# Other seeds for the plan that gives the large buffers of a two-layer generator block their SBUF addresses

## The chip, the cores and the metric

The kernel is one program on one core of one Trainium2 chip. The metric is the device time of one execution in microseconds (us); lower is better.

## The reference

Two layers run over 512 latent tokens and 256 context tokens of width 1024, all in 32-bit floats. A layer has two halves:

```
h = modulate(rmsnorm(x)); p = h @ w_in            # q, k, v, pooling and Fourier inputs, four gates
y = neighbourhood attention, differential attention, pooling mixer, Fourier mixer
x = x + gt1 * (sum_i sigmoid(gate_i) * (y_i @ w_br[i])) @ w_o
h2 = modulate(rmsnorm(x)); aff = softmax(h2 @ w_router)
each of 16 experts takes its top 64 latent (32 context) tokens:
x = x + gt2 * scatter_add(g * (silu(xe @ w_gate) * (xe @ w_up)) @ w_down)
```

The last layer drops the context's own mixers and experts. An expert's weights are 3 x 1024 x 1408 floats, 17.3 MB, and are read once per layer.

## The kernel before, in words

Work is traced once without addresses to find out in which order instructions read and write each large buffer. The program is then traced a second time with an address for every large buffer ("Q" tile: weights, raw loads, attention heads, residuals, accumulators). All of them live in one arena of 183296 bytes per partition (L56). Between the two traces a planner (`place`, `place_part`, `fit`, L60 to L125) chooses the addresses. Small tiles come from ordinary pools and are not part of the plan.

The planner knows of each buffer its first and last instruction and its size. `fit` gives a buffer the place whose latest former user ended earliest in the list of instructions, among the places that are free over its whole life; expert weights (22528 bytes, or halves of 11264) go to multiples of their size. `place_part` takes the buffers of one stretch in an order: first those that live for 2000 instructions or more, then by first use. A buffer that finds no place is moved forward at a position that a random generator with the given seed draws, up to 400 times. `place` does this for four stretches in turn, divided by the marks that the program sets: layer 0 up to its second expert's loads; the experts of layer 0 and the start of layer 1; layer 1 from the end of its first projection to its second expert's loads; the experts of layer 1. Each has its seed in `SEEDS` (L57); where that seed finds no placement, seeds 0 to 39 are tried.

An address works on the time through waits alone: the first write into a place waits for the last user of what lay there. For a load that wait is taken by the queue that issues it, and everything behind it on that queue waits too. SP issues most loads, in program order: raw gate weights `craw` (L598), raw output weights `wo_raws` (L402), attention heads (L769 and L770, with POOL; L887 and L888, with ACT), residuals `x_res` (L1408), and expert weights `w_ex` (L1440 for the first ones, the head; L1445 for the rest).

The head is the first expert's gate and up weights in eight quarter loads (A, A, A, A, B, B, B, B), two blocks of the second expert's (1A) and two of the first expert's down weights (0D). They lie end to end over 180224 of the arena's 183296 bytes, and each takes the place of something that the output projection still uses. In layer 1 four of them are issued before the output projection's first pass (L1204), among the loads of `x_res` and `wo_raws`; one more at the start of its second pass (L1380), the others behind it. `queued` (L1429) lets no more than two expert loads be in flight. After the second pass come top-k on VectorE, a gather of token rows by POOL (L1485), the experts' gate and up products (`gu`, L1512, inputs c = 0 to 7, A holds 0 to 3, B 4 to 7) and down products (L1545). The next expert's block takes a place as soon as the two input slices that lay there have been used.

Of the kernel before, what the change touches and what calls it, by code (L numbers as in the profile page):

```python
# [53 lines left out]


ARENA = 183296  # L56
SEEDS = 48, 0, 1, 0  # L57


def lifetimes(instructions, asked):  # L60
# [10 lines left out]
def fit(lives, room, offs, n):  # L71

    a, z, size = lives[n]
    near = [(offs[m], offs[m] + lives[m][2], *lives[m][:2]) for m in offs]
    busy = [(p, e) for p, e, f, t in near if f <= z and t >= a]
    some = {0, room - size} | {e for _, e, _, _ in near} | {p - size for p, _, _, _ in near}
    best = None
    for o in range(0, room - size + 1, size) if size in (4 * WB, 2 * WB) else sorted(some):
        if o < 0 or o + size > room or any(o < e and p < o + size for p, e in busy):
            continue  # L80
        key = max((t for p, e, f, t in near if t < a and p < o + size and o < e), default=-1), o
        if best is None or key < best:
            best = key
    return best and best[1]


def place_part(lives, room, part, seed, done, tries=400):

    rnd = random.Random(seed)
    order = sorted(part, key=lambda n: (lives[n][1] - lives[n][0] < 2000, lives[n][0]))  # L90
    for _ in range(tries):
        offs = dict(done)
        for n in order:
            o = fit(lives, room, offs, n)
            if o is None:
                break
            offs[n] = o
        else:
            return offs
        order.remove(n)  # L100
        with_n = [i for i, m in enumerate(order) if m in offs and lives[m][0] <= lives[n][1] and lives[m][1] >= lives[n][0]]
        order.insert(rnd.choice(with_n) if seed and with_n else 0, n)


def place(lives, room, marks):


    done = {}
    for z, (a, b) in enumerate(zip([0] + marks, marks + [len(lives)])):
        for seed in (SEEDS[z], *range(40)):  # L110
            offs = place_part(lives, room, range(a, b), seed, done)
            if offs is not None:
                break
        else:
            raise ValueError("no room")
        done = offs
    return [done[n] for n in range(len(lives))]
# [1700 lines left out]
```

## Time and profile before

| | |
|---|---|
| median of 3 runs | 2738.1 us (2737.04 to 2740.97) |
| the profiled execution | 2742.23 us, span 2740.4 us |
| TensorE (PE) busy | 2429.4 us, 89% of the span |
| VectorE, ScalarE, GpSimd busy | 983.3, 577.4, 474.3 us |
| HBM read and written | 734.01 and 39.58 MB |

A row of the profile gives an engine, a line of the kernel, the tiles written and read, a count and times in us. "PE x <- DMA y" in a list of waits says that PE stood idle before x until the transfer y had landed. SPq, ACTq and POOLq are the queues' own instructions.

### The profile page before, as it was taken

How to read it: one execution, taken by the hardware profiler on the slowest of the kernel's cores; microseconds unless marked ns; L12 is line 12 of the kernel's file. 1: busy time of each engine (PE TensorE's matmuls, PEld its weight loads, DVE VectorE, ACT ScalarE, POOL GpSimd, SP SyncE). 2: the span in 40 equal slices, each digit the busy share in tenths (PEclk: the TensorE clock that was granted, in tenths of full speed). 3: DMA queues.
4: the chain of work that ended last, by engine and by line, in shares of the span. 5: the costliest groups of instructions: out<-in, count | busy, mean ns of one | idle time of the engine just before them, and what ended most of it. 6: DMA issues, size and time to landing. Idle time of an engine off the chain costs nothing. (4 is left out here: it accounts for less than half of the span.)

```text
span 2740.4 us, 48684 instructions
## 1 busy us (share of the span) xinstructions
PE 2429.4 (89%) x21446; PEld 1679.8 (61%) x21446; DVE 983.3 (36%) x1986; ACT 577.4 (21%) x1094; POOL 474.3 (17%) x347
## 2 busy tenths in 40 slices
PE   7989889999969999999997799999974977777776
PEld 5778889999845555677774677877862422222222
DVE  5666547643251111111112765477432110110101
ACT  4324445433310000000001424344320000000000
POOL 1352332211240111111001211011121111010100
PEclk9999999999989999999998899999996999999999
DMA  7673552323379999999997575544369999999997
GB/s 291 194 246 121 174 167 63 104 82 102 118 301 421 414 415 411 412 414 409 414 413 285 171 233 162 170 127 129 119 208 370 420 419 422 417 419 420 419 418 324
DMA packets 131154, 776.74 MB, mean 283 GB/s; under 512 B 13312, under 2 KB 51072, under 8 KB 107136
## 3 DMA queue, kind: packets, MB, share of 16 engines
q1 hardware_dynamic: 113296, 730.38, 68.5%
q0 software_dynamic: 11776, 25.44, 3.9%
q10 hardware_dynamic: 5872, 17.83, 2.1%
q8 instruction: 168, 2.75, 0.4%
q14 instruction: 42, 0.34, 0.0%
HBM read 734.01 MB, written 39.58 MB: 282 GB/s over the span
## 5 line engine op out<-in xcount | busy, mean ns | idle before, releaser
L1512 PE MATMUL gu_ps<-w_ex,xT 128*32 128x352 f32 x10240 | 815.8, 472 | 131.1 <-DMA w_ex<-in_w_ex 93.7
L1512 PEld LDWEIGHTS gu_ps<-w_ex,xT 128*32 128x32 f32 x10240 | 469.9, 112 | 471.2 <-issue 227.0
L616 PE MATMUL gate_ps<-hh,cw 128*128 128x384 f32 (+1 forms) x1536 | 456.2, 364 | 8.7 <-ACT sg L1010 4.6
L1545 PE MATMUL dn_ps<-w_ex,hidT 128*32 128x512 f32 x2816 | 343.7, 596 | 36.9 <-DMA w_ex<-in_w_ex 34.7
L616 PEld LDWEIGHTS gate_ps<-hh,cw 128*128 128x128 f32 x1536 | 287.5, 192 | 34.3 <-issue 5.4
L1521 ACT ACTIVATE hid<-gu_ps 128x352 f32<-128x352 f32 x80 | 37.1, 464 | 1282.4 <-PE gu_ps L1512 1282.4
L616 PE MATMUL gate_ps<-hl,cw 128*128 128x384 f32 (+1 forms) x768 | 277.8, 362 | 0.0
L1545 PEld LDWEIGHTS dn_ps<-w_ex,hidT 128*32 128x32 f32 x2816 | 115.7, 110 | 232.3 <-issue 192.5
L1547 DVE SCALAR_TENSOR_TENSOR y_e<-dn_ps,gval,gt 128x512 f32<-128x512 f32 x32 | 24.0, 751 | 471.2 <-PE dn_ps L1545 471.2
L1522 DVE TENSOR_TENSOR hid<-hid,gu_ps 128x352 f32<-128x352 f32 x80 | 41.7, 521 | 355.8 <-ACT hid L1521 246.6
L616 PEld LDWEIGHTS gate_ps<-hl,cw 128*128 128x128 f32 x768 | 147.6, 192 | 10.6 <-issue 1.5
L173 DVE TENSOR_TENSOR cw<-craw,cw 128x1280 fp32r<-128x1280 f32 (+1 forms) x72 | 116.8, 1626 | 31.2 <-ACT cw L172 30.8
L1526 POOL DMA_INDIRECT out<-y_e,idx x16 | 25.8, 1609 | 586.4 <-DVE y_e L1547 586.4
L1539 DVE SCALAR_TENSOR_TENSOR y_e<-dn_ps,gval,gt 128x256 f32<-128x256 f32 x16 | 7.7, 484 | 308.9 <-PE dn_ps L1537 308.9
L1030 POOL TENSOR_TENSOR acc<-acc,sg 128x384 f32<-128x384 f32 (+1 forms) x48 | 62.5, 1302 | 321.9 <-DVE sg L1020 223.0
L1526 POOL DMA_INDIRECT cs<-y_e,idx x16 | 27.1, 1691 | 494.0 <-DVE y_e L1539 494.0
L1537 PE MATMUL dn_ps<-w_ex,hidT 128*32 128x256 f32 x1408 | 99.5, 379 | 0.0
L172 ACT CAST cw<-craw 128x1280 fp32r<-128x1280 f32 (+1 forms) x72 | 88.9, 1240 | 38.2 <-PE branch_ps L1014 11.0
L282 POOL TENSOR_TENSOR ada_acc<-ada_acc,w_ada_k 128x1024 f32<-128x1024 f32 x28 | 71.5, 2554 | 130.0 <-ACT w_ada_k L281 129.9
L284 DVE SCALAR_TENSOR_TENSOR ada_acc<-w_ada_k,scT,ada_acc 128x1024 f32<-128x1024 f32 x56 | 81.0, 1446 | 33.0 <-DMA w_ada_k<-in_w_ada 31.2
L1010 ACT ACTIVATE sg<-gate_ps 128x384 f32<-128x384 f32 (+1 forms) x96 | 50.5, 526 | 177.6 <-PE gate_ps L616 148.8
L909 DVE TENSOR_REDUCE df_m<-df_s 128x1 f32<-128x768 f32 (+1 forms) x80 | 66.9, 845 | 34.4 <-PE df_s L908 34.3
(347 smaller groups left out, 3198.2 us busy)
## 6 DMA issues: line engine op xcount, KB each, us to landing
w_ex<-in_w_ex SPq DMA_DIRECT2D x176, 2816.0 KB
w_ada_k<-in_w_ada SPq DMA_DIRECT2D x80, 512.0 KB
craw<-in_w_gb SPq DMA_DIRECT2D x64, 640.0 KB
w_ex<-in_w_head SPq DMA_DIRECT2D x16, 1408.0 KB
w_ex<-in_w_head SPq DMA_DIRECT2D x8, 2816.0 KB
qkv_raws<-in_w_qkv SPq DMA_DIRECT2D x12, 768.0 KB
w_ada<-in_w_ada SPq DMA_DIRECT2D x4, 2048.0 KB
wo_raws<-in_w_out SPq DMA_DIRECT2D x8, 768.0 KB
```

The costliest lines, as they stand in the source:

```text
L172: self.nc.scalar.copy(hi, src)
L173: self.nc.vector.tensor_sub(lo, src, hi.bitcast(F32))
L282: nc.gpsimd.tensor_add(a, a, t)
L284: nc.vector.scalar_tensor_tensor(a, t, sc, a, op0=OP.mult, op1=OP.add)
L616: nc.tensor.matmul(ps, w[:, lw, k], self.hT(lh, k, t0, t1), start=(k == 0 and s == 0), stop=(k == 7 and s == 2))
L909: nc.vector.tensor_reduce(st[:, m:m + 1], sp[:, 0:n], axis=AX.X, op=OP.max)
L1010: nc.scalar.activation(sg, pg, AF.Tanh, scale=0.5)
L1030: nc.gpsimd.tensor_add(ac, ac, sg)
L1512: nc.tensor.matmul(PG[e, g][s][32 * j:32 * j + 32], XT[e][:, g, c], self.w_gu(e, c, s, j), start=(c == 0), stop=(c == 7))
L1526: nc.gpsimd.indirect_dma_start(out=x, out_offset=bass.IndirectOffsetOnAxis(ap=idx, axis=0), in_=y, in_offset=None, compute_op=OP.add)
L1537: nc.tensor.matmul(ps[32 * j:32 * j + 32], HT[e][:, 2, k], self.w_dn(e, k, 256 * j, 256 * j + 256), start=(k == 0), stop=(k == 10))
L1545: nc.tensor.matmul(ps[32 * q:32 * q + 32], HT[e][:, g, k], self.w_dn(e, k, 512 * h, 512 * h + 512), start=(k == 0), stop=(k == 10))
```

## The change

Two constants and one sort key. The first and the third of the four seeds change; the second and the fourth stay. With an even seed the order in which buffers are placed starts as before (long-lived first), with an odd seed it starts by first use alone. No instruction of the program is added, removed or moved by the text of the change.

```
 ARENA = 183296
-SEEDS = 48, 0, 1, 0
+SEEDS = 150, 0, 27, 0
...
     rnd = random.Random(seed)
-    order = sorted(part, key=lambda n: (lives[n][1] - lives[n][0] < 2000, lives[n][0]))
+    order = sorted(part, key=lambda n: (seed % 2 == 0 and lives[n][1] - lives[n][0] < 2000, lives[n][0]))
     for _ in range(tries):
```

## Rows read from the trace of the kernel before

**Rows 1.** The page, part 1: busy us and share of the span.
```profile
span 2740.4 us, 48684 instructions
PE 2429.4 (89%) x21446; PEld 1679.8 (61%) x21446; DVE 983.3 (36%) x1986; ACT 577.4 (21%) x1094; POOL 474.3 (17%) x347
```

**Rows 2.** Windows: length, engines' busy us, then clock, DMA share, GB/s.
```profile
823.30:1450.00 626.70, 625.73 (x8229) 407.35 (x8225) 100.86 (x161) 20.42 (x44) 80.10 (x64) 1.00 1.01 414
2101.50:2713.60 612.10, 482.96 (x5267) 183.72 (x5259) 67.36 (x105) 13.90 (x30) 47.47 (x39) 0.96 1.01 420
...
763.00:811.00 48.00, 25.93 (x231) 15.67 (x229) 29.98 (x89) 6.66 (x14) 17.08 (x14) 0.79 0.83 321
2041.50:2101.50 60.00, 23.01 (x180) 15.74 (x183) 21.60 (x72) 5.68 (x13) 20.07 (x14) 0.63 0.88 340
```

**Rows 3.** PE's waits, whole span: us in total, times, longest.
```profile
PE na_s L796 <- DMA na_head<-na_st: 7.3, 3, 3.7
PE df_s L907 <- DMA df_head<-df_st: 4.1, 1, 4.1
PE wo_ps L1380 <- ACT wo_w L172: 9.1, 1, 9.1
PE wo_ps L1380 <- DVE wo_w L173: 0.9, 1, 0.9
```

**Rows 4.** SP's waits, 1640 to 1722 and 1760 to 1786 us.
```profile
SPq L769 <- PE poolw_ps L687: 5.8, 1, 5.8
...
SPq L769 <- PE fnet_wps L739: 4.6, 1, 4.6
...
SPq L887 <- PE branch_ps L1014: 4.8, 1, 4.8
```

**Rows 5.** Timeline of SP, 1900 to 2140 us: start, us, issue.
```profile
1959.33 0.38 SPq L402 DMA_DIRECT2D wo_raws<-in_w_out  x1
1971.65 0.38 SPq L1440 DMA_DIRECT2D w_ex<-in_w_head  x1
1975.99 5.02 SPq L1408 DMA_DIRECT2D x_res<-xs  x8
1981.06 21.68 SPq L1440 DMA_DIRECT2D w_ex<-in_w_head  x3
2002.84 0.94 SPq L402 DMA_DIRECT2D wo_raws<-in_w_out  x2
...
2020.86 63.80 SPq L1440 DMA_DIRECT2D w_ex<-in_w_head  x8
```

**Rows 6.** SP's waits, 1959 to 2013 us.
```profile
SPq L1440 <- DMA w_ex<-in_w_head: 17.6, 1, 17.6
...
SPq L1440 <- PE gate_ps L616: 11.9, 1, 11.9
...
SPq L1408 <- PE branch_ps L1014: 3.9, 1, 3.9
```

**Rows 7.** SP's waits, 2013 to 2102 us.
```profile
SPq L1440 <- PE wo_ps L1380: 24.8, 2, 20.2
```

**Rows 8.** Windows of 5 us, columns as in rows 2.
```profile
1965.00:1970.00 5.00, 5.00 (x24) 4.14 (x23) 1.38 (x2) 0.75 (x2) 0.00 (x1) 1.00 0.00 0
...
2030.00:2035.00 5.00, 5.00 (x27) 3.91 (x27) 3.18 (x5) 1.31 (x4) 1.51 (x2) 1.00 0.03 13
```

**Rows 9.** The page, part 6: size of one quarter load of the head.
```profile
w_ex<-in_w_head SPq DMA_DIRECT2D x16, 1408.0 KB
```

**Rows 10.** POOL's waits, 1980 to 2130 us.
```profile
POOL xg L1485 <- DMA h2s<-h: 24.1, 1, 24.1
```

**Rows 11.** SP's waits, 630 to 830 us.
```profile
SPq L1440 <- PE wo_ps L1380: 32.3, 1, 32.3
```

**Rows 12.** Timelines of SP (2060 to 2105 us) and of PE (2085 to 2130 us).
```profile
2099.72 5.07 SPq L1445 DMA_DIRECT2D w_ex<-in_w_ex  x2
...
2091.80 22.07 PE L1512 MATMUL gu_ps<-w_ex,xT 128*32 128x352 f32 x256 [20.89 <-issue]
```

## The prediction

> **What bounds the kernel now.** I first read the page's first part [rows 1]: TensorE is busy for 89% of the span, but that is a mean over stages with different limits, so I cut the span into windows. In both expert stages (the first two windows of [rows 2]) the 16 DMA engines are busy all the time (share 1.01, at 414 and 420 GB/s) over 627 and 612 us. What follows the moment at which such a stream runs full has a fixed length: those bytes at that rate. In between, TensorE is the busy engine, and a layer's way to its stream is TensorE's work plus its gaps. So a gain must come from one of two things: less idle time of TensorE ahead of a stream, or less idle time of the DMA engines in the run-up to it (the last two windows of [rows 2]): 0.17 of 48 us is 8.2 us in layer 0, 0.12 of 60 us is 7.2 us in layer 1.
>
> The list of TensorE's waits says which gaps an address can have caused. An address acts only through a load that waits for its place. Of the causes in that list, four can be of this kind [rows 3]: attention heads of the neighbourhood branch landing late (7.3 us in three waits), differential heads (4.1 us), and output weights that came late to be split (9.1 and 0.9 us). Together 21.4 us. The other waits are for results of VectorE, ScalarE or POOL, or lie inside the full streams, and no address removes them.
>
> **The change, part by part.** The text adds and removes no instruction. It moves buffers, and each moved load counts by what it waits for, on the queue that it holds up.
>
> *Attention heads.* In layer 1 the first head loads stood in SP's queue until TensorE had finished with the buffers that lay there: 5.8 us for the pooling product, 4.6 us for the Fourier product, 4.8 us for a branch product [rows 4]. These users end just before the heads are needed, so a place that came free longer ago would let the load go that much earlier. Bounds: nothing, if the new places end as late, and 7.3 + 4.1 = 11.4 us [rows 3], if all four gaps close. No row says how many close; I take the middle, **5.7 us**.
>
> *Output weights of layer 1.* SP issues a `wo_raws` load at 1959.3, then stands until 1971.65 with the first quarter of the head (11.9 us, for a gate product), then until 1975.99 with `x_res` (3.9 us, for the last branch product), then puts out three more quarters; the last of these waits 17.6 us for an earlier quarter to land, since only two may be in flight [rows 5, 6]. Only then, at 2002.84, come the next two `wo_raws` loads, and TensorE stands still for 10.0 us in front of the second pass [rows 3]. If the new plan frees `x_res` alone, everything behind it moves up by 3.9 us. If it also frees the first quarter, the DMA engines, which do nothing at 1965 to 1970 [rows 8], take it then, and the whole stall can go. If it frees only the quarter, nothing moves, as `x_res` still holds the queue. Bounds 0 and 10.0; I take the smaller of the two gains, **3.9 us**.
>
> *Head loads behind the output projection, layer 1.* At 2020.86 the fifth quarter goes out and the sixth then waits 20.2 us for a product of the second pass [rows 5, 7], while the DMA engines are nearly idle (0.03 at 2030 to 2035) [rows 8]. Counting sizes in the code, the second pass keeps three `acc_r`, three `wo_w`, two `x_res` and one `rows` of 12288 bytes, 110592 in all; six quarters of 11264 fit beside them, so the sixth need not wait. Its 1408 KB [rows 9] are 1.44 MB, and at 420 GB/s [rows 2] they take 3.4 us out of the busy run-up. POOL's gather waits 24.1 us for a store of token rows to land [rows 10], which looks like more to win; but an earlier gather only brings forward loads that find the DMA engines busy, so the bound is their idle time, 7.2 us. Bounds 0 and 7.2; I take **3.4 us**. [...]
>
> *Layer 0.* There the second pass keeps four `acc_r`, three `wo_w`, two `x_res` and two `rows`: 135168 bytes. Beside them exactly four quarters fit, and the fifth must wait for the pass to end: its 32.3 us wait for a product of that pass [rows 11] stays under any plan. Bounds 0 and the 8.2 us of idle DMA time; I take **0**.
>
> *New waits.* The buffers that make room must lie elsewhere, and the arena is nearly full. A new wait can cost nothing, where another engine's work covers it, up to the price of the slower rival below (7.3 us). The nearest row is the mean head wait, 7.3 / 3 = 2.4 us [rows 3]; I take one such, **2.4 us lost**.
>
> Sum: 5.7 + 3.9 + 3.4 - 2.4 = 10.6 us gained. Against the profiled execution, 2742.2, that makes 2731.6; that execution lies 4.1 us above the median of the runs shown, so against 2738.1 the forecast is 2727.5 us.
>
> **The rivals.**
>
> *All of it goes.* 21.4 us of gaps and 7.2 us of idle DMA time close: 28.6 us, giving 2709.5. For it: every one of these waits names a buffer's late user. Against it: the planner counts instructions and not microseconds, and the arena is full at the end of each output projection, whatever the order.
>
> *The waits change their tile.* Each place that is free early for one load is taken from another, and the total stays: 2738.1. This is also what comes out if the change doesn't do what it says: if seed 150 or 27 finds no placement in 400 tries, the seeds 0 to 39 are tried and an arbitrary plan results; and the planner's order of instructions need not be that in which the queues reach them.
>
> *Slower: halves that do not pair.* The streams' first full blocks need two neighbouring quarters of the head. Now the first block of layer 1 goes out at 2099.72 and both are out by 2104.79, 5.07 us later [rows 12], as soon as the gate and up products have used inputs 0, 1 and then 2, 3. If the new plan sets an A quarter beside a B quarter, the first block waits for input 4. TensorE ends the eight inputs at 2091.80 + 22.07 = 2113.87 [rows 12]; the last four take (2113.87 - 2104.79) / 4 = 2.27 us each, so input 4 is done at 2107.1, 7.3 us after 2099.7, and the whole stream moves back: 2745.4 if nothing else changes. It decides as soon as the second quarter's neighbour is one of B. For it: quarters go to any multiple of 11264 bytes, and nothing in the planner asks for pairs. Against it: quarters that come free together tend to be neighbours.
>
> **How the numbers follow.** A part of the waits goes, as summed: 0.42. All of it: 0.10. No net change: 0.25. Slower, by pairs that fail or by a wait of that size: 0.23. The forecast is the likeliest case, 2727.5; its own range runs from 2716.7 (all 21.4 us of TensorE's gaps) to 2732.6 (5.5 us). The range for all, 2711 to 2748, reaches to just short of the case in which all goes, and takes in the slower case with one new head wait on top (2745.4 + 2.4). About 0.2% (5.5 us) is what a measurement of this kernel can tell from no change. Faster by more than that: the first two cases, 0.52. Within it: 0.25. Slower: 0.23.
>
> **What would show it.** Right: in the list of TensorE's waits the rows for `na_head` and `df_head` shrink to about half, the wait for `wo_w` to about 6 us; SP issues `x_res` of layer 1 without a wait for a branch product; the sixth quarter goes out near 2021 less the shift; both expert streams keep share 1.01 and their lengths. Wrong: a new wait of TensorE for a load that now has none; SP held before a `craw` or `wo_raws` load by a late user; the first full block of a stream waiting for a gate product later in the order; or an order of instructions on PE, DVE or ACT other than before, since then the gaps would be new ones and the sum would be about another program.

## The result and the profile after

The changed kernel took 2726.5 us (median of five runs, 2720.9 to 2729.5) beside 2741.0 for the kernel before (median of five): ratio 0.9949, 95% interval [0.9931, 0.9966], 14.5 us faster. The forecast was 2727.5, a gain of 10.6 us. The profiled execution, 2720.94 us, is the fastest of the five.

First the page of the changed kernel, part 1, then all waits of TensorE, over the whole span, that the forecast had counted.

```profile
span 2719.1 us, 48675 instructions
PE 2412.0 (89%) x21446; PEld 1666.4 (61%) x21446; DVE 979.0 (36%) x1986; ACT 577.8 (21%) x1094; POOL 469.0 (17%) x347
```

```profile
PE wo_ps L1380 <- ACT wo_w L172: 6.9, 1, 6.9
PE na_s L796 <- DMA na_head<-na_st: 4.9, 1, 4.9
...
PE wo_ps L1380 <- DVE wo_w L173: 2.0, 2, 1.1
```

The work is the same (21446 products), but TensorE is busy for 17.4 us less than in [rows 1]. Of the 21.4 us of waits in [rows 3], 13.8 are left: the row for differential heads is gone, the neighbourhood heads wait once (in layer 0) instead of three times, the output weights still cost 6.9 us in one piece. So 7.6 us of waits went, and the two profiled spans differ by 21.3. To find the rest, the span is cut at events that all kernels have (the start of what is called first and the end of what is called last, in the trace; us):

| stretch | before | before, mirrored | changed | changed, mirrored |
|---|---|---|---|---|
| start to layer 0's first full block (L1445) | 823.4 | 820.1 | 818.2 | 819.7 |
| to layer 0's last gate and up product | 650.0 | 651.9 | 652.1 | 651.6 |
| to layer 1's first pooling product | 158.0 | 159.3 | 155.7 | 162.0 |
| **mixers**: to layer 1's last gate product | 343.2 | 342.8 | 327.4 | 325.9 |
| **output and run-up**: to layer 1's first full block | 125.2 | 122.5 | 125.1 | 127.3 |
| to the end | 640.7 | 641.9 | 640.6 | 640.8 |

(The mirrored kernels are the first experiment: the same programs once more.) By the means of the two executions each, the mixers of layer 1 gain 16.4 us, layer 0's way to its stream 2.8, the output stage of layer 1 loses 2.3, and the rest stays within 1 us. The windows of the mixers, first of the kernel before, then of the changed one (length, then busy us of PE, PEld, DVE, ACT, POOL, then clock, DMA share, GB/s):

```profile
1631.34:1974.56 343.22, 328.72 (x1660) 260.31 (x1659) 208.29 (x426) 143.92 (x270) 51.54 (x42) 0.98 0.47 144
```

```profile
1625.98:1953.39 327.41, 322.03 (x1660) 255.09 (x1659) 208.25 (x426) 143.65 (x269) 49.96 (x42) 1.00 0.49 149
```

The same 1660 products: idle time falls from 14.5 to 5.4 us, and the products themselves take 6.7 us less, at a granted clock of 1.00 instead of 0.98. Three stretches at half clock account for nearly all of that: in the kernel before, TensorE's granted clock stood at 0.50 for 3.4 us from 1678, 10.2 us from 1784 and 3.4 us from 1876 us, and it was busy for 13.8 us of them. Products of 128x512 started every 0.43 us there (1791 to 1793 us) and every 0.23 us at a clock of 1.00 (1794 to 1797 us), so that 13.8 x (1 - 0.23/0.43) = 6.4 us are lost to the lower clock, an estimate from these rows; the changed kernel's mixers have no such stretch. The forecast had priced idle time alone.

In the output stage SP's timeline of the changed kernel, and two of its waits from 1917 to 2085 us, answer to [rows 5 to 7]:

```profile
1953.19 5.42 SPq L1408 DMA_DIRECT2D x_res<-xs  x8
1958.72 21.10 SPq L1440 DMA_DIRECT2D w_ex<-in_w_head  x4
1979.91 0.95 SPq L402 DMA_DIRECT2D wo_raws<-in_w_out  x2
...
1997.78 62.86 SPq L1440 DMA_DIRECT2D w_ex<-in_w_head  x8
2078.51 60.27 SPq L1445 DMA_DIRECT2D w_ex<-in_w_ex  x10
```

```profile
SPq L1408 <- PE gate_ps L616: 28.4, 1, 28.4
SPq L1440 <- PE wo_ps L1380: 20.8, 1, 20.8
```

SP now stands 28.4 us at the residual rows until the last gate product, while the DMA engines are nearly idle (share 0.07 from 1925 to 1953 us); everything else is issued behind them, and the sixth quarter waits 20.8 us for a product of the second pass, where it waited 20.2. POOL's wait for the stored token rows, of [rows 10], got longer:

```profile
POOL xg L1485 <- DMA h2s<-h: 27.0, 1, 27.0
```

So most of the time comes from one place, the attention heads of layer 1, and from more than their waits.

### The profile page after: what moved, and what is told of

Its sections match the earlier page's. It is cut to its first block, busy times and chain, and to the rows that moved or that the text cites. A ratio compares the mean times of both kernels' runs of the same rounds, so it can differ in the third digit from the quotient of the medians.

```text
span 2719.1 us, 48675 instructions
## 1 busy us (share of the span) xinstructions
PE 2412.0 (89%) x21446; PEld 1666.4 (61%) x21446; DVE 979.0 (36%) x1986; ACT 577.8 (21%) x1094; POOL 469.0 (17%) x347
## 5 line engine op out<-in xcount | busy, mean ns | idle before, releaser
L1545 PEld LDWEIGHTS dn_ps<-w_ex,hidT 128*32 128x32 f32 x2816 | 114.6, 110 | 238.7 <-issue 200.4
L284 DVE SCALAR_TENSOR_TENSOR ada_acc<-w_ada_k,scT,ada_acc 128x1024 f32<-128x1024 f32 x56 | 73.7, 1316 | 38.3 <-DMA w_ada_k<-in_w_ada 38.1
L1537 PEld LDWEIGHTS dn_ps<-w_ex,hidT 128*32 128x32 f32 x1408 | 62.8, 109 | 24.0 <-issue 2.2
```

Of the source, the lines that this page charges most:

```text
L284: nc.vector.scalar_tensor_tensor(a, t, sc, a, op0=OP.mult, op1=OP.add)
L1537: nc.tensor.matmul(ps[32 * j:32 * j + 32], HT[e][:, 2, k], self.w_dn(e, k, 256 * j, 256 * j + 256), start=(k == 0), stop=(k == 10))
L1545: nc.tensor.matmul(ps[32 * q:32 * q + 32], HT[e][:, g, k], self.w_dn(e, k, 512 * h, 512 * h + 512), start=(k == 0), stop=(k == 10))
```

## The experiments

All plans below are lists of offsets, written into the kernel in place of the planner's answer:

```
-    nc, arrays = build(io_arrays, place(lives, ARENA, marks))
+    nc, arrays = build(io_arrays, PLAN)
```

### Do the bytes themselves matter, and how far does an execution scatter?

```
PLAN[n] = ARENA - plan_before[n] - lives[n][2]
```

> The kernel before with every large buffer moved from offset o to the end of the arena minus o minus its size. Every pair of buffers that shared bytes still does, and the order of the instructions is the same on all five engines. Theory (an address acts only through the wait of a load for its place): 2738 us within 4, ratio to before 0.998 to 1.002, and the same rows in the waits of TensorE, each within 1 us. Rival (the bytes themselves matter, by a bank or a port): off by more than 0.2%, with unequal durations of equal instructions. Beside that, the half-clock stretches of TensorE between 1640 and 1980 us are looked at: if they stand elsewhere than in the trace of before, with the same program, part of the 21.3 us between the two profiled executions is the draw of the execution, and not the change.

Measured: 2738.8 us, ratio 0.9995 [0.9983, 1.0006]. The same overlaps at other bytes take the same time. The stretches are those of the table above; none moves by more than 3.2 us. TensorE's clock between 1640 and 1980 us falls at the same three places as before (0.50 from 1785.0 to 1793.3 us; 0.97 over the mixers, beside 0.98). One expectation missed: the waits did not keep to 1 us. TensorE's waits for `na_head` sum to 3.4 us instead of 7.3, since the longest, 3.7 us, is 1.9 us here and put down to ScalarE; the mixers took as long (342.8 us).

> The changed kernel mirrored in the same way: the same overlaps, the same order of instructions on every engine. Theory: 2726 us within 4, ratio to before 0.993 to 0.997. It is a second look at the changed program: if its profiled execution again shows granted clock 1.00 from the first head product of layer 1 to the last gate product, the full clock there belongs to the change; if stretches at half clock turn up, it was luck.

Measured: 2728.8 us, ratio 0.9972 [0.9960, 0.9984], a smaller gain (10.0 us) than the changed kernel's own 0.9949 (14.5 us), with intervals that just meet, and a hair outside the 0.993 to 0.997 that was expected. By the table the 8.0 us between the two profiled executions lie mostly in layer 1's projections (6.3 us), and order and overlaps are equal there, so 6 us, and not 3.2, is the scatter by which any one stretch must be read. The mixers are as short as in the changed kernel (325.9 us, clock 1.00), so that gain and its full clock belong to the change and not to chance.

### Each seed alone

```
PLAN[n] = plan_after[n] if n < 221 else plan_before[n]
```

> Addresses of the changed kernel for the buffers asked for up to layer 0's gathers (seed 150), those of before from layer 1 on (seed 1, long-lived first). Theory (each seed acts on its own layer): layer 0's first full block goes out near 818.2 us instead of 823.4, layer 1's way from its last expert product of layer 0 to its own first full block stays at 626 us, 2733 to 2736 us in all. Rival (the order of instructions, which is worked out anew, carries the gain over into the other layer): layer 1's way shortens by more than 5 us as well.

(Buffers 0 to 220 are layer 0's, its expert stream with them. In the other half before and after change places.) Measured: 2735.6 us, ratio 0.9988 [0.9977, 1.0000]. Layer 0's first full block goes out at 822.8 us, not near 818.2 as expected, and layer 1's mixers take 340.3 us, as before within the scatter. Layer 1's way is 620.2 us, beside 626.4 in the trace of before and 624.6 in the mirrored one: 4 to 6 us shorter, no more than the scatter, so that the rival isn't excluded.

> The other half: addresses of before for layer 0 (seed 48), those of the changed kernel from layer 1 on (seed 27). Theory: layer 0's first full block near 823.4 us as before, layer 1's way 608 to 612 us instead of 626, 2724 to 2729 us in all; with the other half the two gains add up to the change's. Rival (the gain is one of both together, or sits in layer 0): under 5 us of gain here.

Measured: 2734.8 us, ratio 0.9990 [0.9979, 1.0001]: a miss, since 2724 to 2729 was expected. The mixers did come down, to 326.5 us, but the way to the first pooling product grew to 166.5 us. This pairing of halves has a wait of its own. SP's timeline before, and in this kernel:

```profile
1459.52 0.90 SPq L402 DMA_DIRECT2D qkv_raws<-in_w_qkv  x2
...
1489.67 0.33 SPq L1410 DMA_DIRECT2D xq<-cs  x1
```

```profile
1487.93 0.33 SPq L1410 DMA_DIRECT2D xq<-cs  x1
1488.35 0.86 SPq L402 DMA_DIRECT2D qkv_raws<-in_w_qkv  x2
```

The first two projection weights go out behind the token rows, at which SP stands for 27.2 us, and no longer ahead of them. ScalarE starts to split those weights at 1498.8 us instead of 1476.3. So the shorter mixers are layer 1's seed alone. That this load, with its late turn in the queue, costs all of the 8 us is not shown: the same stretch scattered by 6.3 us at equal order. On this chip the halves gain 3.2 and 4.0 us, and both together, mirrored, 10.0; within the intervals they add up.

### The places or the order of the instructions?

The scheduler that orders the engines' instructions knows the places, so a new plan also gives a new order, and the traces of before and changed do differ in it on all five engines. Two kernels cross them: TensorE and POOL are chained, without any wait for an end, to the order of the other kernel.

```
+    for e, name in order:
+        if e in (mybir.EngineType.PE, mybir.EngineType.Pool,) and name in here:
+            if e in last and (name not in region or region.get(last[e]) != region[name]):
+                tc.add_manual_dep(here[name], last[e], mybir.DependencyInfo(
+                    mybir.DependencyClass.NoSync, mybir.DependencyReason.DATA), reason="order")
+            last[e] = name
```

> Addresses of before; TensorE's and POOL's instructions are held to the order that they have in the changed kernel, the other engines' are worked out anew. Theory (the places themselves bring the gain): the head loads still wait, the stretch of layer 1 from the first pooling product to the last gate product stays near 343 us (343.2 before, 327.4 after), 2736 to 2742 us in all, ratio 0.999 to 1.002. Rival (the other order of TensorE's instructions, which came with the new plan, brings it): that stretch under 333 us, 2724 to 2731 us in all.

> The other way round: addresses of the changed kernel, TensorE and POOL held to the order that they have before. Theory (places): that stretch of layer 1 326 to 330 us, 2724 to 2732 us in all. Rival (order): near 343 us, 2736 to 2742 us in all.

Measured: 2771.0 us, ratio 1.0119 [1.0099, 1.0138], with the old places, and 2754.8 us, 1.0064 [1.0047, 1.0081], with the new ones: both slower than either kernel, and neither theory as it stood. TensorE's waits in the mixers of layer 1 say why; first old places under the new order, then new places under the old order (of the second list the three longest rows):

```profile
PE na_s L796 <- DMA na_head<-na_st: 12.1, 2, 6.1
PE df_s L907 <- DMA df_head<-df_st: 11.1, 2, 6.9
```

```profile
PE df_s L907 <- ACT df_p L912: 9.4, 6, 3.0
PE df_rt L971 <- DVE df_m L910: 1.7, 1, 1.7
PE df_tp L933 <- ACT df_at L935: 1.6, 2, 1.4
```

The new order asks for the heads earlier; over the old places they are then 23.2 us late in all, where the kernel before lost 8.6, and the mixers take 363.7 us. Under the old order the new places do remove every wait for a head there, but TensorE stands idle for 16.5 us, nearly all of it for the softmax on ScalarE and VectorE, and the mixers take 343.9 us, with nothing gained. Five kernels with these places and the order that the scheduler makes for them take 325.9 to 327.9 us. A likely reason, not shown, is that heads that are there early let the scheduler start them early (the first differential product stands 135.1 us behind the first pooling product instead of 149.4), and more gate products are then left to put between the softmax steps.

One limit is large: the other engines' order was worked out anew in these two kernels. In the second one's mixers only 315 of VectorE's 426 instructions stand in the sequence of the kernel before, fewer than the changed kernel's 347, and the 16.5 us are waits for just these engines. In layer 0 both kernels are late too (first full block at 831.2 and 830.8 us, beside 823.4 and 818.2), the second with a wait of 10.9 us for a differential head. So the head waits are the places' doing, but whether TensorE's new order is needed for the gain stays open.

### What does a wait cost beyond its own length?

In the two long waits for heads of the kernel before, products that nobody reads keep TensorE busy; the order of all engines is held.

```
-                H = heads[h2]
+                H = self.busy(heads, h2, (l, pair, u) == (1, 0, units[1]), 1, 15)
...
-                H = heads[h2]
+                H = self.busy(heads, h2, (l, pair, u) == (1, 0, units[1]), 2, 17)
...
+    a, b = heads[0][:, 0, 0:128], heads[0][:, z, 0:T]
+    ps = self.TP("busy_ps")
...
+    for _ in range(n):
+        self.nc.tensor.matmul(ps, a, b, start=True, stop=True)
```

Windows of the kernel before behind those two waits, and of this kernel behind the products that fill them:

```profile
1678.52:1683.00 4.48, 4.48 (x16) 3.80 (x17) 2.41 (x10) 2.13 (x5) 0.00 (x0) 0.69 0.68 266
...
1785.69:1794.00 8.31, 7.63 (x22) 5.71 (x23) 6.87 (x12) 5.63 (x9) 1.29 (x1) 0.50 0.26 93
```

```profile
1680.67:1685.15 4.48, 4.48 (x25) 3.85 (x24) 3.00 (x14) 2.21 (x5) 0.00 (x0) 1.00 0.70 256
...
1786.40:1794.70 8.30, 6.30 (x29) 4.55 (x30) 8.22 (x17) 5.66 (x9) 1.29 (x1) 1.00 0.29 93
```

> The kernel before, all engines held to its order, with products that nobody reads in TensorE's two longest waits for a head load in layer 1: 15 in the 3.67 us ahead of 1678.5, 17 in the 4.11 us ahead of 1785.7, each 0.23 us at full clock, so that they end before the load lands. The waits themselves stay. Theory (a wait costs its idle time and after it a stretch at half clock: 0.69 granted in the 4.5 us behind the first, 0.50 in the 8.3 us behind the second): the clock stays at 1.00 behind both, the stretch from the first pooling product to the last gate product shortens by 4 to 7 us from 343, the whole by as much. Rival (the price of a wait is its idle time alone): no change, that stretch 342 to 344 us; or the products delay the heads' own and it gets longer by up to 3 us.

Measured: 2739.2 us, ratio 0.9996 [0.9985, 1.0007]; mixers 340.6 us. The clock did what was expected, 0.69 and 0.50 became 1.00, so the fall does follow from TensorE standing still ahead of it. The size was a miss: the mixers gained 2.5 us, not 4 to 7, no more than one stretch scatters, and the whole nothing that can be measured. The order is the kernel before's, so its products can be compared one by one, counted from the first pooling product. They run 1.5 us earlier behind the first wait and 3.1 behind the second; 0.4 is lost again at the third fall of the clock, near 1875 us, behind a wait for the softmax that this kernel does not fill (6.8 us at half clock instead of 3.4). The second window shows why it gave back so little: 29 products instead of 22, but VectorE is busy for 8.22 of the 8.30 us, and TensorE, at full clock, stands idle for 2.0 us, most of it for the softmax. An estimate from the kernel before's trace: TensorE was busy at 0.50 for 2.8 us behind the first wait and for 7.6 us behind the second, and by the 0.43 and 0.23 us from one product's start to the next's that is 1.3 and 3.5 us lost to the lower clock. The comparison agrees with it behind the first wait (1.5) and not behind the second (1.6), where the softmax was the next bound.

### The forecast's two other terms, each tried by itself

**Output weights.** In the changed kernel they stand in SP's queue behind four quarters.

```
+        if self.wname == "wo_w" and n in (3, 4) and len(self.big) > 20:
+            self.tc.add_manual_dep(self.big[{3: -4, 4: -2}[n]], ins.ins.name, mybir.DependencyInfo(
+                mybir.DependencyClass.NoSync, mybir.DependencyReason.DATA), reason="order")
```

> The changed kernel with one edit in the order of SP in layer 1: the fourth load of output weights goes ahead of the head's first quarter and the fifth ahead of the third; addresses are the changed kernel's. Theory (what is left of the stall in front of the second pass, 6.9 + 0.9 us of waits for weights, comes from those loads standing behind four quarters, and half clock follows it): the stall is under 1 us, the granted clock behind it 1.00, the second pass starts and ends 8 to 13 us earlier, and the end too, 2713 to 2720 us. Rival (the quarters, now later, or the run-up of the stream take it back): second pass earlier, first full block of the stream not, 2724 to 2729 us.

Measured: 2725.2 us, ratio 0.9950 [0.9935, 0.9965], the changed kernel's time, as the rival had it. TensorE's waits from 1955 to 2030 us:

```profile
PE wo_ps L1380 <- ACT wo_w L172: 5.0, 1, 5.0
PE wo_ps L1380 <- DVE wo_w L173: 1.3, 2, 1.0
```

The second pass starts 7.1 us earlier after the last gate product (29.6 instead of 36.6), and takes 41.1 us instead of 35.5, because the next weights are late (the 5.0 us). Weights, rows and quarters all cross the DMA engines after the last gate product (share 0.83 from 1960 to 1989 us); turning them round helped one and hurt another.

**The residual rows.** So they must be out before.

```
PLAN[324] = 73728
```

(the residual tile with the first three groups of rows; in the changed kernel 24576. There a gate's weights ended three gates earlier; 36 other buffers make room, and the stream's blocks follow.)

> Other places for 37 buffers from the last differential heads of layer 1 on, so that the first of the two residual tiles lies where a gate's weights ended three gates earlier. In the changed kernel SP stands 28.4 us in front of these rows until the last gate product, and all that the output projection needs next stands behind it. Theory (the forecast's term for the output weights, with the queue as its mechanism): the rows are issued at least 8 us before the last gate product, the wait for output weights in front of the second pass falls from 7.8 us to under 4, the end comes 3 to 6 us earlier, 2721 to 2726 us. Rival (the first quarter of the head waits for the last gate product all the same, and the loads behind it are bound by the DMA engines): rows early, stall unchanged within 2 us, 2725 to 2730 us.

Measured: 2718.8 us, ratio 0.9928 [0.9908, 0.9947]. SP's timeline of this kernel:

```profile
1942.86 0.38 SPq L402 DMA_DIRECT2D wo_raws<-in_w_out  x1
1945.88 3.79 SPq L1408 DMA_DIRECT2D x_res<-xs  x6
1955.40 0.39 SPq L1440 DMA_DIRECT2D w_ex<-in_w_head  x1
...
1971.72 0.95 SPq L402 DMA_DIRECT2D wo_raws<-in_w_out  x2
...
1992.49 68.14 SPq L1440 DMA_DIRECT2D w_ex<-in_w_head  x8
2071.04 13.98 SPq L1445 DMA_DIRECT2D w_ex<-in_w_ex  x3
```

Six of the eight row loads go out from 12 us before the end of the last gate product (1958.1). TensorE's wait for output weights is 0.4 us, the second pass takes 32.0 us, at clock 1.00 throughout, and the stretch from the last gate product to the first full block is 113.0 us, beside 125.1 and 127.3. Of these 13 us some 8 are given back: the mixers are 4 to 5 us longer (331.3; TensorE waits 2.6 us for a load in front of a differential product there, and 3.4 us at half clock follow), and the stream takes 644.3 us, since its first block now finds the head's loads unfinished (SP waits 16.2 us for them). It is the fastest place-only version here.

> Both edits: the residual rows early, and the fourth and fifth load of output weights ahead of the head's first and third quarter. With the weights first alone the first part of the stall went (6.9 to 0.3 us) and came back at the next weights (6.0 us), since rows, quarter and weights all crossed the DMA engines after the last gate product. Theory (what bounds this stage is the bytes that can't start before the last gate product): with the rows out of the way both waits fall under 2 us together, the second pass ends 6 us earlier than in the changed kernel, 2718 to 2724 us. Rival (the full clock or the run-up takes it back): stall gone, end not earlier than with the weights first alone, 2724 to 2729 us.

Measured: 2721.0 us, ratio 0.9922 [0.9907, 0.9938]. No wait for weights is left, and the stretch is 109.4 us; the end is no earlier than with the rows alone, within the interval, and by the medians earlier than with the weights first alone. Both versions with early rows are faster than the kernel before. Their medians, 2718.8 and 2721.0 us, also lie below those of the changed kernel and of its other versions (2725 to 2729), but one by one the intervals still meet.

**The sixth quarter.**

```
PLAN[336], PLAN[337] = 123904, 112640
```

> The changed kernel with other places for 23 buffers around the output projection of layer 1, so that the fifth and the sixth quarter of the head lie where nothing is needed any more when SP comes to them; the order of TensorE differs in two places only. In the changed kernel SP still waits 20.8 us for a product of the second pass with the sixth quarter, as before (20.2). Theory (the DMA engines' idle time in the run-up is worth what the forecast said): the sixth goes out about 20 us earlier, the last head loads land 3 us earlier, the first full block and the end come 2 to 4 us earlier, 2721 to 2726 us. Rival (the first full block waits for the gate and up products, which wait for the gather of the tokens and not for quarters): the sixth goes out early, the first full block does not move by more than 1 us, 2725 to 2730 us. Second rival: the early transfers push back the output weights or the token rows, 1 to 4 us slower.

(The two halves of a block that nothing in the second pass uses; 101376 and 90112 in the changed kernel. 21 other buffers make room.) Measured: 2726.0 us, ratio 0.9948 [0.9931, 0.9964]. The sixth quarter went out 47 us behind the last gate product instead of 66, and the seventh then waited 25.0 us for the second pass. The stretch to the first full block: 126.5 us, as in the changed kernel. TensorE's waits from 1955 to 2085 us say what it depends on:

```profile
PE gu_ps L1512 <- DVE xT L1494: 21.7, 1, 21.7
```

The first rival: the gate and up products wait for the gathered tokens, not for quarters. A quarter landing earlier is worth nothing while the tokens come last.

## Why the prediction came out right

The total was right to 1 us, but as a sum of terms that missed on both sides, and with some luck. The forecast of 10.6 us was set against a median of 2738.1; the five runs beside the result have 2741.0, so the gain was 14.5 us there, and 10.0 in the mirrored kernels.

- **What bounds the kernel**: right. The streams kept their lengths (652 and 641 us), and the gain lies in TensorE's way to the second one.
- **Attention heads, 5.7 us**: the mechanism was right, the size was not; this is the term that failed most. All 8.6 us of layer 1's waits went (5.3 in the mirrored kernels), layer 0's grew from 2.8 to 4.9, and the mixers gained 16.4, above the upper bound of 11.4. The bound counted idle time only. In the two windows of the mixers 9.1 us of the gain are idle time and 6.7 us are the products themselves, which no longer ran at half clock (6.4 us by the estimate above). With the head waits filled only some 2.5 us of that came back, since the softmax was the next bound and the third fall of the clock stayed. In the changed kernel the softmax waits did not grow although the heads were there (5.3 us in the mixers, 5.8 before); whether that is the work of the new order, no run separates.
- **"No address removes them"**, said of the waits for VectorE and ScalarE: wrong. Places act on the order too, and with the order of the engines these waits ran, in the mixers, from 4 us (changed, mirrored) to 16 us (new places, old order).
- **Output weights, 3.9 us**: did not come. The stall went from 10.0 to 7.8 us in the changed kernel, but from 9.3 to 10.6 between the mirrored ones, and the stretch got 2.3 us longer. The text named the condition, `x_res` free before the last products, and the new plan doesn't meet it (28.4 us of wait). Where a plan meets it, the stretch takes 113.0 us, 10.9 less than in the kernel before, nearly three times the term: the rows were the head of the queue, and all that the output stage needs stood behind.
- **Sixth quarter, 3.4 us**: did not come, and by the one run that tries it would have been worth nothing. The step that failed is the one that took idle DMA time in the run-up for lost time; the gather of the tokens comes later. It does count once the rest is early: in the kernel with early rows the first block waits for the head's loads.
- **Layer 0, 0 us**: 2.8 by two executions each. Over all kernels but the two crossed ones, layer 0's first full block goes out at 818.2 to 822.8 us with the new half (seven) and at 820.1 to 824.7 with the old (four), so about 2, with ranges that overlap.
- **New waits, 2.4 us lost**: of that size, inside the stretches above: 2.1 us more for a head in layer 0 (5.0 in the mirrored kernels), and 2.9 us more of POOL's wait for the stored rows. Why those stores come later was not separated.
- **The rivals**: "the waits change their tile" describes the output stage well and the mixers not at all. "Halves that do not pair" could not happen: the first two full blocks are written in the program ahead of the products of the second four inputs, so a block over an A half and a B half would destroy what is still to be read, and no plan may place it. As far as the 0.23 rested on it, it should have got no chance.
- **The sign of error that the text named**, an order of instructions other than before, did occur, and the gaps were new ones, as it said. That the total still fitted is partly luck: heads too small by 10.7, weights and quarter too large by 9.6.

## What to carry to other kernels

When a scheduler sees the addresses, a plan is judged with its order: in the mixers here places that were free earlier paid twice, once for the waits (9.1 us less idle time) and once for the clock behind them (6.7 us less for the same products), and holding two engines to an order made for other places cost more than the change brings (1.0119 and 1.0064). In a stage where one queue issues everything, look for the load at its head that waits longest (here 28.4 us for rows that the DMA engines, at a share of 0.07, could have fetched), not for the wait that the busy engine shows. And ask of every transfer brought forward what the next stage waits for last.

## What the runs showed of the hardware

After TensorE stood still for 4.1 us its granted clock was 0.50 for the next 8.3 us, and it stayed at 1.00 when the same time was filled with products that nobody reads. At 0.50 products of 128x512 started every 0.43 us, at 1.00 every 0.23 us. The second pass of layer 1, the same products, took 32.0 us where it began at a granted clock of 1.00 behind a wait of 0.4 us, and 35.1 to 35.9 in the four executions of the first table, behind a wait of 7.8 to 10.6 us (mean granted clock 0.91 before and 0.90 in the changed kernel). In two executions with equal order and equal overlaps (the changed kernel and its mirror) the projections of layer 1 took 155.7 and 162.0 us: a few us in one stretch of one trace show nothing.
